# A fourth split weight tile in the place of the activations, and one more block with another order of products

## The chip, the cores and the metric

One Trainium2 chip, one of its cores. The metric is the device time of one execution of the whole kernel in microseconds (us). Engines: PE = TensorE, DVE = VectorE, ACT = ScalarE, POOL = GpSimd, SP = SyncE; PEld is the loading of weights into TensorE.

## The reference

The kernel computes one decoder layer, all in float32: 256 tokens and 16 meta tokens in front of them, 2048 channels. An attention half and a pooling half are mixed and normalised; then comes a gated feed-forward part with 5632 channels, whose time this text is about:

```
h = layer_norm(ALPHA * h + mix, ln1_g, ln1_b)
z = h @ w_up                                  # 2048 -> 2 x 5632
z = causal depthwise conv of width 3 over the tokens, + conv_b
a, g = split(z, 2)
f = (gelu(a) * g) @ w_down                    # 5632 -> 2048
h = layer_norm(ALPHA * h + f, ln2_g, ln2_b)   # meta tokens are dropped
```

## The kernel before

**Weights.** All weights come as tiles of 128 partitions and 2048 float32 columns, 1 MB each, in one list, `stream`. A float32 matmul is done as three products of a faster format: each operand is written as an upper part (rounded) and a lower part (the rest), and the products upper·upper, upper·lower and lower·upper are added. So each tile is loaded by SP's queue (L190) into a raw buffer `wraw`, ACT copies its upper part into a split buffer `whl` (L184), and DVE subtracts that from the raw tile for the lower part (L185). A tile is split in two or three parts (`cuts`): 512 and 1536 columns for a tile of `w_up`, 1024 and 1024 for an A tile of `w_down`, 1024, 512 and 512 for a B tile. There are three raw and three split buffers (pool `wp`). `weights` hands out the next tile and emits the work for tiles up to two ahead.

**Feed-forward part.** `ffn_plan` lists the work. A tile of `w_up` ("up") makes one block of 128 output channels: 16 steps of three products with 258 columns each, 48 in all (L295). `b` counts these blocks, from -8; `lead(b)` says in which order the three products of a step come in the first step: "l" is the lower part of the weights by the upper part of the activations, "x" the upper part by the lower, "h" upper by upper. Two up blocks (a and g) pass through `conv` (ACT L824, DVE L825 and L826) and `gate` (ACT L841, DVE `za` L842). A tile of `w_down` is used in a scheme of seven block products instead of eight: an A tile takes part in four of them, a B tile in three, each with three matmuls of 512 columns (`seven`, L893 to L895), so 12 and 9. Four A tiles, then four B tiles, and so on in turn; up tiles and down tiles alternate one by one. The seven products need sums of blocks of the weights (DVE L196 for an A tile, L200, L201, L202 for a B tile, made in the raw buffer) and of the activations: `forms` makes the latter on POOL after every second pair of blocks (L866 to L869, in the program's text s[0], s[2], s[1], s[3]), and `two_parts` splits them (ACT L847, DVE L848; tiles `gp` and `right`).

**PSUM.** The up blocks use the four buffers of pool `pm`, the down products the four of `pa` (tile `at`). At the end of four A tiles ACT copies two sums (`u` L907, `v` L909) and DVE adds two to the output (`y<-y,at`, L903); at the end of four B tiles DVE does `y<-y,v`, `u` (L917), `y<-y,at` and `v` (L918). POOL's queue then adds `u` and `v` to the output with accumulating transfers (L912, L913; L920 to L922). These two places are called hand-overs here, from A to B and from B to A tiles.

**Order.** The instructions of each engine run in order. That order is set when the kernel is built, by a scheduler that takes the program's dependences, the free buffers and its own idea of durations; `issue_after` in the text adds edges that it must keep.

**The place.** The tile of tag "y" first holds x, then the normalised activations. After the normalisation, 32 transfers (`residual`, L817, on ACT's queue, called from the loop over the plan) move these to the output's buffer `y2`; the list of those still to come is `moves`. After that nothing uses the place until tile number `spare`, near the end of the stream, whose split tile `whl_y` lies there.

Of the kernel before, what the change touches and what calls it, by code (L numbers as in the profile page):

```python
# [12 lines left out]
F32R = mybir.dt.float32r  # L13
# [4 lines left out]
P = 128  # L18
# [84 lines left out]

def lead(b):

    if 8 < b < 16:
        return (), ("lxh",)
    return (), ()

# [14 lines left out]
def places(n):  # L124

    upper, apart, turned = WAYS[(n >= 8) + (n >= 26) + (n >= 26 + KT)]
    return upper, upper + apart, turned
# [8 lines left out]
def tile_layer(ctx, tc, xt, w_first, w_proj, w_uk, w_uv, w_pool, w_o, w_up, w_down, cols, rows, rel_bias, onehot, out):  # L136
    nc = tc.nc
    sb = ctx.enter_context(tc.tile_pool(name="sb", bufs=1))
# [23 lines left out]
    kinds, leads, downs_at = {}, {**{i: LEAD_X for i in (10, 14)}, **{26 + m: LEAD_H for m in (0, 1, 5)}}, {}  # L162
# [12 lines left out]
    spare, last = len(stream) - PARTS[-1], len(stream) - 1  # L175
    VALUES = stream.index(w_uv)
    ready, raws, split, held = {}, {}, {}, []
    state = {"next": 0, "use": 0}

    def split_part(raw, hl, c, after=()):  # L180
        with ExitStack() as edges:
# [6 lines left out]
    def fetch(raw, hl, src, kind, front, at_up=False):  # L188

        nc.sync.dma_start(raw, src)  # L190
        b11, b12, b21, b22 = (raw[:, c:c + 512] for c in range(0, 2048, 512))
        cuts = (0, 1024, 2048)
        if kind == "A":

            with tc.issue_after(front):
                nc.vector.tensor_tensor(b12, b12, b11, op=ALU.subtract)  # L196
        if kind == "B":

            with tc.issue_after(front):
                nc.vector.tensor_tensor(b12, b22, b12, op=ALU.subtract)  # L200
            nc.vector.tensor_tensor(b11, b12, b11, op=ALU.add)  # L201
            nc.vector.tensor_tensor(b21, b21, b11, op=ALU.subtract)  # L202
            cuts = (0, 1024, 1536)
        if hl.lead is not None or kind is None and at_up:
            cuts = (0, hl.first or 512, 2048)
        for a, b in zip(cuts, cuts[1:]):
            parts = split_part(raw, hl, slice(a, b))
        return parts

    def split_tile(where=(0, 2048)):  # L210

        return Split(wp.tile([P, 4288], F32R, tag="whl", name="whl"), *where)

    def weight_tiles(where):
        raw = wp.tile([P, 2048], F32, tag="wraw", name="wraw")
        return raw, split_tile(where)

    def emit(i):
        if i in ready:
            return  # L220
        if i == last:

            raw = wp.tile([P, 2048], F32, tag="wraw", name="wraw")
            nc.sync.dma_start(raw, stream[i])
            raws[i] = raw
            ready[i] = []
            for c in range(0, 2048, 256):
                hl = ring.tile([P, 2, 258], F32R, tag="act", name="whl_r", padded_shape=[P, 2, WIDE])
                nc.scalar.activation(hl[:, 0, :256], raw[:, c:c + 256], AF.Copy)
                nc.vector.tensor_tensor(hl[:, 1, :256], raw[:, c:c + 256], hl[:, 0, :256].bitcast(F32), op=ALU.subtract)  # L230
                ready[i].append(hl)
            return
        if i == spare:
            raw = wp.tile([P, 2048], F32, tag="wraw", name="wraw")
            hl = Split(sb.tile([P, 4160], F32R, tag="y", name="whl_y"), 0, 2056)
        else:
            raw, hl = weight_tiles((0, 2112) if i > spare else downs_at.get(i, places(i)) + leads.get(i, ()))
        ready[i] = hl
        if i == VALUES:

            nc.sync.dma_start(raw, stream[i])
            held.extend((raw, hl))
            return
        split[i] = fetch(raw, hl, stream[i], kinds.get(i), i and i - 1 in split and split[i - 1][1], i in orders)
        if i >= spare:
            raws[i] = raw
# [6 lines left out]
    def weights(ahead=2):  # L253
        i = state["use"]
        state["use"] += 1
        prefetch(i + 1 + ahead)
        return ready.pop(i)
# [44 lines left out]
    for k0, k1 in [(k, k + 1) for k in range(9)] + [(9, 12), (12, 15), (15, 16)]:  # L302
        if k0 == KT - 1:

            raw = ap_.tile([P, 1024], F32, name="wraw_l", tag="v1")[:, :T + MF].rearrange("p (a b) -> p a b", a=1)
        elif k0 % 3 == 0:
            raw = wp.tile([P, 2048], F32, tag="wraw", name="wraw")
            raw = raw[:, :3 * (T + MF)].rearrange("p (a b) -> p a b", b=T + MF)
        if k0 % 6 == 0:
            hl = split_tile()  # L310
# [155 lines left out]
    for j in range(8):  # L466
        hl = weights()
# [39 lines left out]
    y = sb.tile([P, KT, T], F32, tag="y", name="x", padded_shape=[P, KT, T])  # L507
# [50 lines left out]
    for h in range(H):  # L558
        hl = weights()
# [127 lines left out]
    for h in range(H):  # L687
# [3 lines left out]
        hl = weights()  # L691
# [121 lines left out]
    def residual(a, b, i):  # L813

        src, dst, t = slice(32 * a, 32 * a + 32), slice(32 * b, 32 * b + 32), NM + i * P + 32 * b
        to = y2[dst, i, :].rearrange("p (m d) -> p m d", d=P)[:, :, src]
        nc.scalar.dma_start(to, y[src, :, t:t + 32])  # L817

    turns = list(range(KT))
    moves = [(a, b, i) for i in range(2) for a in range(4) for b in range(4)]  # L820
# [106 lines left out]
    for item in plan:  # L927
        if item[0] in "AB":
            seven(*item)
            continue  # L930
        if item[0] == "down":
            _, part, c, g = item
            hl = weights()
            if c == 1:
                emit((last, spare)[g])
                if g == 0:
                    row_sums(last, ready[last])
            if g == 0:
                downs = [big(), big()]
            n = PARTS[part]  # L940
            for k in range(4 * g, 4 * g + 4):
                w = slice(512 * (k - 4 * g), 512 * (k - 4 * g) + 512)
                for i in range(2):
                    a, r = pairs[part][k // 2][f"a{i + 1}{k % 2 + 1}"]
                    nc.tensor.matmul(downs[i], a[:, 0, r], hl[:, 0, w], start=k == 0, stop=False)
                    nc.tensor.matmul(downs[i], a[:, 0, r], hl[:, 1, w], start=False, stop=False)
                    nc.tensor.matmul(downs[i], a[:, 1, r], hl[:, 0, w], start=False, stop=k == n - 1)
            if g == n // 4 - 1:
                for i in range(2):
                    yc = y2[:, i, 512 * c:512 * c + 512]  # L950
                    nc.vector.tensor_tensor(yc, yc, downs[i], op=ALU.add)
            continue
        _, f, half_ = item
        part = next(p for p in range(len(PARTS)) if f < sum(PARTS[:p + 1]))
        if half_ == 0:
            if f % 2 == 0:
                pair = fp.tile([P, 2, S], F32, name="za", tag="z0", bufs=3)
            both = []
        hl = weights()
        ps = big()  # L960

        b = 2 * (f - FOLDED) + half_
        upper, lower = split[state["use"] + 1]
        with tc.issue_after(lower):
            for m in turns[:(0, 5, 5, 6)[b] if 0 <= b < 4 else 0]:
                nc.vector.transpose(y[:, m, NM:], y[:, m, NM:])
                turns.remove(m)
        with tc.issue_after(upper):
            for _ in range(0 if b < 4 else 4 if b < 8 else 3):
                if moves:  # L970
                    residual(*moves.pop(0))
        if todo and f > FOLDED + half_:
            p, r = todo.pop(0)
            with behind(state["use"]):
                pairs[p].append(forms(r, len(pairs[p]), p == FAST))
        if f < FOLDED:
            k = 0
            if f + half_ == 0:
                product(ps[:, :NE], hl, folded, 0, NE, K_UP, k1=5)
                deviation()  # L980
                k = 5
            product(ps[:, :NE], hl, folded, 0, NE, K_UP, k0=k)
            with behind(state["use"]):
                while len(h_parts) < min(KT, 2 * (2 * f + half_ + 1) + 3):
                    normalise(len(h_parts))
            both.append(ps)
            if half_ == 0:
                continue
            both = [conv(i * FT + f, i, unfold(both[i]), pair[:, f % 2]) for i in range(2)]
        else:  # L990
            product(ps[:, :NQ], hl, h_parts, 0, NQ, K_UP, ks=late_last if f == FOLDED else None,
                    firsts=orders[state["use"] - 1])
            both.append(conv(half_ * FT + f, half_, ps, pair[:, f % 2]))
            if half_ == 0:
                continue
        gate(*both)
        if part > FAST:
            a = fp.tile([P, 2, WIDE], F32R, name="gp", tag="gp", bufs=16)
            gated.append(two_parts(a[:, :, :S], both[0]))
        elif f % 2:  # L1000
            todo.append((part, pair))
# [192 lines left out]
```

## Time and profile before

| | us |
|---|---|
| Runs, median of 3 | 1021.62 (1021.62 to 1033.16) |
| Profiled execution, its own time | 1020.11 |
| Its span, first to last instruction | 1018.3 |
| PE busy | 1011.5 |
| DVE busy | 889.9 |
| ACT busy | 621.2 |

The mean granted clock of TensorE in this execution is 0.997 of full speed. The profile shows one execution: busy times by engine, groups of instructions by line, waits with the engine that ended them, and a timeline. All times further down count from the start of the span. The feed-forward part's alternating stretch lies between about 320 and 965 us. In the timeline, successive instructions of one group stand in one row with their number (x2), and the time is from the first's start to the last's end.

### The profile page before, as it was taken

What the parts mean: (1) busy time and instruction counts of PE and PEld (TensorE: products, weight loads), DVE (VectorE), ACT (ScalarE), POOL (GpSimd) and SP (SyncE); (2) the same over time, 40 slices, a digit from 0 to 9 for tenths busy, and PEclk for the clock granted to TensorE, in tenths of its full rate; (3) what the DMA queues carried; (4) which work ended last, traced back from release to release, by engine and by line L of the source; (5) the groups of instructions that cost most, each with busy time, mean ns of one, the idle gap of its engine ahead of it and who ended that gap; (6) DMA issues with size and microseconds to landing.
All of it is one profiled execution on the core that took longest, in us unless ns stands there. A gap on an engine that the chain in (4) does not pass through costs nothing.

```text
span 1018.3 us, 19199 instructions
## 1 busy us (share of the span) xinstructions
PE 1011.5 (99%) x7644; PEld 963.5 (95%) x7644; DVE 889.9 (87%) x1401; ACT 621.2 (61%) x1000; POOL 187.5 (18%) x245
## 2 busy tenths in 40 slices
PE   9999999999999999999999999999999999999997
PEld 8999999999999999999999999999999999999986
DVE  6878678758879999999998999989999899999976
ACT  7666446655548756655666656656555656565675
POOL 1200014125430021111121111210212102120031
PEclk9999999999999999999999999999999999999998
DMA  8755643354663568979888798878988888888874
GB/s 325 259 190 209 236 156 105 138 196 166 207 207 125 207 208 263 267 291 309 273 288 272 281 302 275 279 262 299 284 269 289 281 296 287 276 291 282 298 229 155
DMA packets 59754, 250.28 MB, mean 246 GB/s; under 512 B 21734, under 2 KB 22416, under 8 KB 32656
## 3 DMA queue, kind: packets, MB, share of 16 engines
q1 hardware_dynamic: 34592, 230.42, 62.8%
q0 software_dynamic: 7888, 16.14, 8.3%
q10 hardware_dynamic: 17184, 2.49, 1.5%
q8 instruction: 60, 0.98, 0.4%
q14 instruction: 30, 0.25, 0.1%
HBM read 232.50 MB, written 2.11 MB: 230 GB/s over the span
## 4 chain that ended last, share of the span: by engine, by line
PE 59%; DVE 20%; DMA 8%; ACT 7%; issue 4%; POOL 1%; SPq 0%; ACTq 0%; POOLq 0%; DVEq 0%
PE mm L295 46%; DVE whl L185 11%; ACT whl L184 6%; DMA wraw<-in_w_up 5%; DMA wraw<-in_w_down 3%; PE at L894 2%; PE at L893 2%; PE at L895 2%; PE mm L366 1%; DVE y L903 1%; DVE wraw L201 1%; DVE wraw L200 1%; DVE wraw L196 1%; DVE gp L848 1%; DMA wraw<-in_w_first 1%
## 5 line engine op out<-in xcount | busy, mean ns | idle before, releaser
L185 DVE TENSOR_TENSOR whl<-wraw,whl 128x1024 fp32r<-128x1024 f32 (+2 forms) x416 | 487.3, 1199 | 51.7 <-ACT whl L184 50.2
L184 ACT ACTIVATE whl<-wraw 128x1024 fp32r<-128x1024 f32 (+2 forms) x416 | 401.9, 1014 | 172.1 <-DVE wraw L201 45.6
L295 PEld LDWEIGHTS mm<-hp,whl 128*128 128x128 f32 x3840 | 456.9, 188 | 6.3
L295 PE MATMUL mm<-hp,whl 128*128 128x258 f32 x3840 | 458.9, 279 | 0.0
L295 PE MATMUL mm<-xp,whl 128*128 128x256 f32 (+5 forms) x1152 | 147.0, 284 | 0.0
L295 PEld LDWEIGHTS mm<-xp,whl 128*128 128x128 f32 x1152 | 140.1, 188 | 1.5 <-issue 0.5
L866 POOL TENSOR_TENSOR forms<-za 128x128 f32<-128x128 f32 x20 | 20.3, 1017 | 294.9 <-DVE za L842 230.2
L894 PE MATMUL at<-whl,gp 128*128 128x512 f32 x180 | 70.6, 393 | 0.0
L895 PE MATMUL at<-whl,gp 128*128 128x512 f32 x180 | 70.4, 392 | 0.0
L893 PE MATMUL at<-whl,gp 128*128 128x512 f32 x180 | 68.7, 392 | 0.0
L869 POOL TENSOR_TENSOR forms<-za 128x128 f32<-128x128 f32 x20 | 19.0, 949 | 201.3 <-DVE za L842 187.5
L824 ACT ACTIVATE z<-mm,cv 128x256 f32<-128x256 f32 x40 | 22.5, 562 | 51.6 <-PE mm L295 51.5
L295 PE MATMUL mm<-mixp,whl 128*128 128x258 f32 x384 | 48.0, 280 | 0.0
L295 PE MATMUL mm<-mixa,whl 128*128 128x258 f32 x384 | 47.2, 279 | 0.0
L295 PEld LDWEIGHTS mm<-mixp,whl 128*128 128x128 f32 x384 | 46.1, 188 | 0.1
L295 PE MATMUL mm<-fold,whl 128*128 128x260 f32 x384 | 45.8, 280 | 0.0
L824 ACT ACTIVATE za<-mm,cv 128x256 f32<-128x256 f32 x40 | 22.4, 561 | 38.1 <-PE mm L295 36.7
L295 PEld LDWEIGHTS mm<-mixa,whl 128*128 128x128 f32 x384 | 45.7, 188 | 0.0
L295 PEld LDWEIGHTS mm<-fold,whl 128*128 128x128 f32 x384 | 45.5, 187 | 0.1
L895 PEld LDWEIGHTS at<-whl,gp 128*128 128x128 f32 x180 | 33.9, 188 | 7.2
L894 PEld LDWEIGHTS at<-whl,gp 128*128 128x128 f32 x180 | 33.8, 188 | 6.1
L893 PEld LDWEIGHTS at<-whl,gp 128*128 128x128 f32 x180 | 33.4, 187 | 6.2
(329 smaller groups left out, 1277.9 us busy)
## 6 DMA issues: line engine op xcount, KB each, us to landing
wraw<-in_w_up SPq DMA_DIRECT2D x88, 1024.0 KB, 5.1
wraw<-in_w_down SPq DMA_DIRECT2D x80, 1024.0 KB, 6.2
wraw<-in_w_proj SPq DMA_DIRECT2D x24, 1024.0 KB, 4.9
wraw<-in_w_o SPq DMA_DIRECT2D x16, 1024.0 KB, 4.8
y<-v POOLq DMA_DIRECT2D x27, 256.0 KB, 8.3
y<-u POOLq DMA_DIRECT2D x18, 256.0 KB, 4.9
wraw<-in_w_first SPq DMA_DIRECT2D x8, 304.0 KB, 5.7
x<-in_xt SPq DMA_DIRECT2D x1, 2176.0 KB, 8.0
```

Source lines behind the costliest of these rows:

```text
L184: upper = nc.scalar.activation(hl[:, 0, c], raw[:, c], AF.Copy)
L185: lower = nc.vector.tensor_tensor(hl[:, 1, c], raw[:, c], hl[:, 0, c].bitcast(F32), op=ALU.subtract)
L196: nc.vector.tensor_tensor(b12, b12, b11, op=ALU.subtract)
L200: nc.vector.tensor_tensor(b12, b22, b12, op=ALU.subtract)
L201: nc.vector.tensor_tensor(b11, b12, b11, op=ALU.add)
L295: nc.tensor.matmul(ps, a, b, start=n == 0 and i == 0, stop=i == 2 and n == KT - 1)
L824: nc.scalar.activation(z, src[:, 2:NQ], AF.Identity, bias=col(C_B, j), scale=col(C_W, 3 * j + 2))
L866: nc.gpsimd.tensor_tensor(s[:, 0], a21, a22, op=ALU.add)
L869: nc.gpsimd.tensor_tensor(s[:, 3], a11, a21, op=ALU.subtract)
L893: nc.tensor.matmul(ps, a[:, 0, i], hl[:, 0, w], start=j == 0, stop=False)
L894: nc.tensor.matmul(ps, a[:, 0, i], hl[:, 1, w], start=False, stop=False)
L895: nc.tensor.matmul(ps, a[:, 1, i], hl[:, 0, w], start=False, stop=j == n - 1)
```

## The change

Two edits. Block 16 gets the order of its first step that the blocks 9 to 15 have. And once the list of moves is empty, a tile `whl_y` of the size of a split buffer is allocated in the place "y"; from then on the split tile of every fourth raw tile is that one instead of one of the three `whl`, up to four tiles before `spare`. In the program that is built, 33 weight tiles have it, each second of the down tiles among them. In the changed file the lines of `fetch` and `split_part` stand one lower (L185 is L186), those of the feed-forward part four lower (L842 is L846, L866 is L870).

```
--- before.py
+++ after.py
@@ -103,7 +103,7 @@
 
 def lead(b):
 
-    if 8 < b < 16:
+    if 8 < b < 17:
         return (), ("lxh",)
     return (), ()
 
@@ -175,7 +175,8 @@
     spare, last = len(stream) - PARTS[-1], len(stream) - 1
     VALUES = stream.index(w_uv)
     ready, raws, split, held = {}, {}, {}, []
-    state = {"next": 0, "use": 0}
+    state = {"next": 0, "use": 0, "raw": 0}
+    more = []
 
     def split_part(raw, hl, c, after=()):
         with ExitStack() as edges:
@@ -211,8 +212,11 @@
 
         return Split(wp.tile([P, 4288], F32R, tag="whl", name="whl"), *where)
 
-    def weight_tiles(where):
+    def weight_tiles(where, i):
         raw = wp.tile([P, 2048], F32, tag="wraw", name="wraw")
+        state["raw"] += 1
+        if more and i < spare - 4 and state["raw"] % 4 == 0:
+            return raw, Split(more[0], *where)
         return raw, split_tile(where)
 
     def emit(i):
@@ -234,7 +238,7 @@
             raw = wp.tile([P, 2048], F32, tag="wraw", name="wraw")
             hl = Split(sb.tile([P, 4160], F32R, tag="y", name="whl_y"), 0, 2056)
         else:
-            raw, hl = weight_tiles((0, 2112) if i > spare else downs_at.get(i, places(i)) + leads.get(i, ()))
+            raw, hl = weight_tiles((0, 2112) if i > spare else downs_at.get(i, places(i)) + leads.get(i, ()), i)
         ready[i] = hl
         if i == VALUES:
 
@@ -969,6 +973,8 @@
             for _ in range(0 if b < 4 else 4 if b < 8 else 3):
                 if moves:
                     residual(*moves.pop(0))
+        if not (moves or more):
+            more.append(sb.tile([P, 4288], F32R, tag="y", name="whl_y"))
         if todo and f > FOLDED + half_:
             p, r = todo.pop(0)
             with behind(state["use"]):
```

The order of instructions on SP and on PE stays, but for the names and block 16. On DVE, ACT and POOL it changes in most of the stretch. First DVE at a hand-over from A to B tiles in the later part of the stretch, before:

```order
L842 TENSOR_TENSOR za<-za,z 128x256
L185 TENSOR_TENSOR whl<-wraw,whl 128x512
L903 SCALAR_TENSOR_TENSOR y_3782<-y_3782,at 128x512 x2
L185 TENSOR_TENSOR whl<-wraw,whl 128x512
L185 TENSOR_TENSOR whl<-wraw,whl 128x1536
L848 TENSOR_TENSOR gp<-za,gp 128x256
L848 TENSOR_TENSOR gp<-forms,gp 128x256
L848 TENSOR_TENSOR right<-forms,right 128x256
L848 TENSOR_TENSOR gp<-za,gp 128x128
```

and after, at the same kind of place:

```order
L829 SCALAR_TENSOR_TENSOR z<-mm,cv,z 128x256
L907 SCALAR_TENSOR_TENSOR y_3782<-y_3782,at 128x512
L830 SCALAR_TENSOR_TENSOR z<-mm,cv,z 128x256
L907 SCALAR_TENSOR_TENSOR y_3782<-y_3782,at 128x512
L846 TENSOR_TENSOR za<-za,z 128x256
L186 TENSOR_TENSOR whl<-wraw,whl 128x512
L186 TENSOR_TENSOR whl<-wraw,whl 128x1536
L852 TENSOR_TENSOR gp<-za,gp 128x256
L852 TENSOR_TENSOR gp<-forms,gp 128x256
L852 TENSOR_TENSOR right<-forms,right 128x256
L852 TENSOR_TENSOR gp<-za,gp 128x128
```

The two adds that read PSUM (`y<-y,at`) stood behind `za`, and a 512 part of an up tile before and behind them; they now stand ahead of `za`, and both parts of the up tile follow it, with `gp` behind them.

DVE at a hand-over from B to A tiles, before:

```order
L842 TENSOR_TENSOR za<-za,z 128x256
L185 TENSOR_TENSOR whl<-wraw,whl 128x1024
L903 SCALAR_TENSOR_TENSOR y_3782<-y_3782,v 128x512
L917 TENSOR_TENSOR u<-u,at 128x512
L903 SCALAR_TENSOR_TENSOR y_3782<-y_3782,at 128x512
L918 TENSOR_TENSOR v<-u,at 128x512
L185 TENSOR_TENSOR whl<-wraw,whl 128x512
L185 TENSOR_TENSOR whl<-wraw,whl 128x1536
L848 TENSOR_TENSOR gp<-za,gp 128x256
L848 TENSOR_TENSOR gp<-forms,gp 128x256
L848 TENSOR_TENSOR right<-forms,right 128x256
```

and after:

```order
L921 TENSOR_TENSOR u<-u,at 128x512
L846 TENSOR_TENSOR za<-za,z 128x256
L922 TENSOR_TENSOR v<-u,at 128x512
L907 SCALAR_TENSOR_TENSOR y_3782<-y_3782,at 128x512
L186 TENSOR_TENSOR whl<-wraw,whl 128x1536
L852 TENSOR_TENSOR gp<-za,gp 128x256
L852 TENSOR_TENSOR gp<-forms,gp 128x256
L852 TENSOR_TENSOR right<-forms,right 128x256
L852 TENSOR_TENSOR gp<-za,gp 128x128
```

`u` moved ahead of `za`; the 1024 part of a down tile and the 512 part of an up tile, which stood behind `za`, are done before it (so is `y<-y,v`, above these rows), and `v` comes ahead of the add. In the changed order `gp` follows two adds and one 1536 part.

POOL over one hand-over of each kind, first from A to B, then from B to A (rows named DMA issue the accumulating transfers), before:

```order
L869 TENSOR_TENSOR forms<-za 128x128
L866 TENSOR_TENSOR forms<-za 128x128
L867 TENSOR_TENSOR forms<-forms,za 128x128
L868 TENSOR_TENSOR forms<-za,forms 128x128
L912 DMA y_3782<-u 128x512
L913 DMA y_3782<-v 128x512
L869 TENSOR_TENSOR forms<-za 128x128
L866 TENSOR_TENSOR forms<-za 128x128
L867 TENSOR_TENSOR forms<-forms,za 128x128
L868 TENSOR_TENSOR forms<-za,forms 128x128
L920 DMA y_3782<-u 128x512
L921 DMA y_3782<-v 128x512
```

and after:

```order
L916 DMA y_3782<-u 128x512
L917 DMA y_3782<-v 128x512
L870 TENSOR_TENSOR forms<-za 128x128
L871 TENSOR_TENSOR forms<-forms,za 128x128
L872 TENSOR_TENSOR forms<-za,forms 128x128
L873 TENSOR_TENSOR forms<-za 128x128
L924 DMA y_3782<-u 128x512
L870 TENSOR_TENSOR forms<-za 128x128
L926 DMA y_3782<-v 128x512
L925 DMA y_3782<-v 128x512
L871 TENSOR_TENSOR forms<-forms,za 128x128
L872 TENSOR_TENSOR forms<-za,forms 128x128
```

L869 (now L873) was the first of its group, far ahead of the others in time since it needs only the first of the two `za`, and is the last; the two transfers at the end of A tiles stand ahead of `forms`, and at the end of B tiles two of the three transfers stand between its first and its second operation.

## Rows read from the trace of the kernel before

**Rows 1.** The page's part 1: busy us (share of the span) x instructions.
```profile
PE 1011.5 (99%) x7644; PEld 963.5 (95%) x7644; DVE 889.9 (87%) x1401; ACT 621.2 (61%) x1000; POOL 187.5 (18%) x245
```

**Rows 2.** Windows: busy us (x instructions) of each engine, PE clock, DMA share, GB/s.
```profile
core 0: us, PE busy (x) PEld busy (x) DVE busy (x) ACT busy (x) POOL busy (x), PEclk, DMA share, GB/s
...
450.00:960.00 510.00, 510.00 (x3734) 481.73 (x3734) 479.74 (x658) 310.44 (x434) 81.97 (x99) 1.00 0.85 285
```

**Rows 3.** Waits of SyncE's queue, whole span: total us, times, longest.
```profile
SPq L190 <- DVE whl L185: 661.6, 165, 13.8
```

**Rows 4.** Waits of DVE, 450 to 960 us.
```profile
DVE whl L185 <- ACT whl L184: 19.4, 44, 2.4
```

**Rows 5.** Waits of ACT, 450 to 960 us.
```profile
ACT gp L847 <- POOL forms L868: 8.6, 11, 1.3
```

**Rows 6.** Timeline, A to B hand-over: start, us, engine, line, operation, count.
```profile
486.56 0.42 DVE L842 TENSOR_TENSOR za<-za,z 128x256 f32<-128x256 f32 x1
...
486.89 0.68 DVE L185 TENSOR_TENSOR whl<-wraw,whl 128x512 fp32r<-128x512 f32 x1
487.06 0.85 POOL L866 TENSOR_TENSOR forms<-za 128x128 f32<-128x128 f32 x1 [14.80 <-DVE za L842]
...
487.50 1.28 DVE L903 SCALAR_TENSOR_TENSOR y<-y,at 128x512 f32<-128x512 f32 x2
...
487.98 0.47 POOL L867 TENSOR_TENSOR forms<-forms,za 128x128 f32<-128x128 f32 x1
488.53 0.46 POOL L868 TENSOR_TENSOR forms<-za,forms 128x128 f32<-128x128 f32 x1
...
489.32 0.41 ACT L847 ACTIVATE gp<-forms 128x256 fp32r<-128x256 f32 x1
...
491.46 0.41 DVE L848 TENSOR_TENSOR gp<-forms,gp 128x256 fp32r<-128x256 f32 x1
```

**Rows 7.** Timeline, B to A hand-over at 840 to 845 us.
```profile
839.64 1.22 DVE L185 TENSOR_TENSOR whl<-wraw,whl 128x1024 fp32r<-128x1024 f32 x1
839.80 1.38 POOL L866 TENSOR_TENSOR forms<-za 128x128 f32<-128x128 f32 x1 [12.15 <-DVE za L842]
...
842.13 0.39 PE L893 MATMUL at<-whl,gp 128*128 128x512 f32 x1
...
842.36 0.39 PE L894 MATMUL at<-whl,gp 128*128 128x512 f32 x1
...
842.84 0.67 DVE L918 TENSOR_TENSOR v<-u,at 128x512 f32<-128x512 f32 x1
...
843.44 2.35 DVE L185 TENSOR_TENSOR whl<-wraw,whl 128x512 fp32r<-128x512 f32 x2
...
843.82 0.85 POOL L921 DMA_DIRECT2D y<-v  x1 [0.33 <-DVE v L918]
...
844.10 1.05 ACT L184 ACTIVATE whl<-wraw 128x1024 fp32r<-128x1024 f32 x1
844.19 0.40 PE L893 MATMUL at<-whl,gp 128*128 128x512 f32 x1
...
844.36 1.20 POOL L922 DMA_DIRECT2D y<-v  x1
...
844.89 1.35 PE L295 MATMUL mm<-hp,whl 128*128 128x258 f32 x10
```

**Rows 8.** Groups of DVE by line and shape, 450 to 960 us: busy, mean ns, idle before.
```profile
L185 DVE TENSOR_TENSOR whl<-wraw,whl 128x1024 fp32r<-128x1024 f32 x96 | 115.7, 1219 | 4.6 <-ACT whl L184 4.1
L185 DVE TENSOR_TENSOR whl<-wraw,whl 128x1536 fp32r<-128x1536 f32 x64 | 113.5, 1774 | 9.1 <-ACT whl L184 8.8
...
L202 DVE TENSOR_TENSOR wraw<-wraw 128x512 f32<-128x512 f32 x32 | 22.0, 688 | 0.9
```

**Rows 9.** Windows of PE alone, up blocks 15 and 16.
```profile
383.31:388.91 5.60, 5.60 (x50) 1.00 0.71 181
388.91:394.57 5.66, 5.66 (x50) 1.00 1.09 288
```

More of the change, by code (lines that the diff above doesn't have):

```diff
@@ L104, in lead @@
 def lead(b):
-    if 8 < b < 16:
+    if 8 < b < 17:
         return (), ("lxh",)
@@ L177, in tile_layer @@
     ready, raws, split, held = {}, {}, {}, []
-    state = {"next": 0, "use": 0}
+    state = {"next": 0, "use": 0, "raw": 0}
+    more = []
     def split_part(raw, hl, c, after=()):
@@ L212, in split_tile, with weight_tiles @@
         return Split(wp.tile([P, 4288], F32R, tag="whl", name="whl"), *where)
-    def weight_tiles(where):
+    def weight_tiles(where, i):
         raw = wp.tile([P, 2048], F32, tag="wraw", name="wraw")
+        state["raw"] += 1
+        if more and i < spare - 4 and state["raw"] % 4 == 0:
+            return raw, Split(more[0], *where)
         return raw, split_tile(where)
@@ L236, in emit @@
         else:
-            raw, hl = weight_tiles((0, 2112) if i > spare else downs_at.get(i, places(i)) + leads.get(i, ()))
+            raw, hl = weight_tiles((0, 2112) if i > spare else downs_at.get(i, places(i)) + leads.get(i, ()), i)
         ready[i] = hl
@@ L971, in tile_layer @@
                     residual(*moves.pop(0))
+        if not (moves or more):
+            more.append(sb.tile([P, 4288], F32R, tag="y", name="whl_y"))
         if todo and f > FOLDED + half_:
```

## Prediction

> **What bounds the kernel now.** I read the page's busy times first: the reader is to see TensorE (PE) at 99% of the span [rows 1]. A share is an average, so next the windows: between 450 and 960 us, the stretch in which up and down tiles alternate and the fourth weight tile works, PE is busy 510.00 of 510 us at full granted clock, and VectorE (DVE) 479.74 [rows 2]. Does late weight data hold PE back there in a way that busy time hides? No: two successive products of 512 columns start at 842.13 and 842.36, 0.23 us apart, 2.2 columns per ns [rows 7]; an up tile has 48 products of 258 columns and takes 5.60 us, again 2.2 per ns [rows 9]. PE streams columns at one rate without gaps. Earlier weights can't make it faster.
>
> Then the waits. SyncE waits 661.6 us for `whl<-wraw` of DVE [rows 3]: the next raw tile is loaded when DVE has finished with one of the three raw buffers. The change adds a split buffer and no raw one, so loads stay paced by DVE. DVE itself is idle 30.3 of the 510 us, and 19.4 of that it waits for ACT's half of a split [rows 4]; the other 10.9 are small waits for loads and `conv`, and hand-offs. So it is nearly a second bound. The timeline shows how near: the row at 843.44 joins the two parts of an up tile's weights, 512 and 1536 columns, and the second leaves DVE at 843.44 + 2.35 = 845.79; PE began that tile at 844.89 [rows 7] and its first twelve products use the first part. It needs the second at 844.89 + 12 × 0.117 = 846.29, half a us later.
>
> **The change part by part.** *Block 16.* Blocks with the first three products as "lxh" take 5.60 us, block 16 without it 5.66 [rows 9]: minus 0.06.
>
> *The fourth split tile.* It takes away a wait of ACT for PE to release a `whl`. In the stretch nothing late hangs on that: SyncE waits for raw tiles [rows 3], and PE for nothing [rows 2]. Gain 0. The 33 tiles at the other address could be read at another rate. The nearest row for such a difference is block 16's 1%; on 33 tiles of 2 to 6 us that is about ±1.5 us. The three addresses of today have one rate, so I take 0. The place's first use must wait for the 32 moves out of it, issued blocks ahead: 0.
>
> *The order.* With a buffer more the scheduler puts the instructions of DVE, ACT and GpSimd (POOL) in another order through the whole stretch, and this can cost. After every four up tiles, in turn at the hand-over from A to B tiles and from B to A, `za` (L842) is followed by `forms` on POOL, their upper parts on ACT (L847) and the lower parts on DVE (L848).
>
> How does POOL fare beside DVE? L866 takes 0.85 us under a DVE split that reads two SBUF operands, ending 0.34 after the split (487.91 against 487.57), and 1.38 under a longer split, ending 0.32 after it. Beside adds that read PSUM, L867 and L868 take 0.47 and 0.46 [rows 6, 7]. A `forms` operation waits out the split. The Trainium skill, "SBUF — State Buffer", section "Who interferes with whom", says that a DVE instruction with two SBUF inputs and a GpSimd instruction that reads SBUF exclude each other for the whole instruction; the trace agrees, 0.85 and 1.38 against 0.46 us. By that rule the sum is the one below; were the access shared, each chain would be about 1 us shorter and the sum some 10 us less.
>
> In the old order, from A to B, two PSUM-reading adds stand behind `za` and POOL's chain runs beside them; `gp<-forms` comes on DVE 491.46 − 486.98 = 4.5 us after `za` ended [rows 6]. In the new order the adds stand ahead of `za`, so behind it come a 512 split, a 1536 split and then `gp`. Counted from `za`'s end: the splits end at 0.70 + 1.77 = 2.5 [rows 6, 8], `gp<-za` at 2.9. POOL: L866 until 0.9 as in the row; L867 starts under the 1536 split and ends 0.33 behind it, 2.8; L868 and L869 follow at the step of 0.55 (488.53 − 487.98), 3.9. L869 stood ahead of the other three, at the `za` before, and is last now, and on ACT `right<-forms` stands ahead of `gp<-forms`: 0.41 each, 4.8 [rows 6]. DVE stands idle from 2.9 to 4.8: 1.9 us. The transfers `y<-u`, `y<-v`, which POOL's queue now has ahead of the chain, can only make it later: 2.0. Behind the waiting DVE instruction stand `right`, the next B tile's combinations and its splits, so every later weight is late by as much.
>
> From B to A two adds (0.67 each [rows 7]) and the 1536 split stand behind `za`: 3.1, and `gp<-za` 3.5. POOL has two transfers between L866 and L867, 0.85 and 1.20 [rows 7], released by `v`. L867 falls under the 1536 split: it ends at 3.4, L869 at 4.5, ACT at 5.3: 1.8 us. If POOL goes on before a transfer is over, 1.4. I take 1.6. Six hand-overs of each kind in the stretch have this order (the first four stay near the old one): 6 × 2.0 + 6 × 1.6 = 21.6 us. Bounds: 0, if `forms` slips in ahead of the splits, and 12 × 2.8, the whole chain after its first 2.0 us.
>
> *B tiles.* The 1024 split now follows L202 directly. ACT's part needs L201 and then 1.05 us [rows 7]; L202 covers 0.69 of it [rows 8], so DVE waits 0.4 us; 32 tiles, 13 us, less the 4.1 that it waits for this form today [rows 8]: 9. In the old order `conv` operations stand between in about half of them. Between 0 and 9 I take 4.5.
>
> *Sum.* DVE's busy time with its 19.4 us for ACT, which come from the order within a tile and stay, is 499.1. Plus 21.6 and 4.5: 525.2 against PE's 510, thus 15.2 over. The other 10.9 us of idle I take to vanish once DVE is behind; if they stay, it is 26. On the profiled execution's 1020.11: 1020.11 + 15.2 − 0.06 = 1035. The median of the runs, 1021.62, is 1.5 us more; a median could stand as much above my number, which the range holds.
>
> **The rivals.** *The cover holds.* The 30.3 us of DVE's idle time absorb the 26.1 of new stalls, since a DVE that is late waits for no one: 479.74 + 26.1 = 505.8, and PE stays at 510: 1020 to 1022. For it: PE waits for nothing today. Against: the 19.4 are for ACT, which itself needs DVE's combinations of the same tile, and half a us of cover at 846.29.
>
> *Slower by more than 2%.* Nothing bends: today's idle stays, all twelve hand-overs cost 2.0 and the B tiles 9: 510 + 24 + 9, so 33 over. From B to A the release of PSUM is late as well: today `v` is read out at 843.51 and PE takes that bank at 844.19, 0.68 later [rows 7]; the new order has `za` and an add ahead of it. With three quarters of this it is 1045, with all 1053. It decides once the new DVE idle that bends nowhere passes 20 us.
>
> *Faster.* If the fourth tile's address reads faster by as much as the order of the first triple saves on a tile, 0.06 us [rows 9], the 33 tiles give 2 us: 1018. The Trainium skill, "Perfetto Trace Analysis", section "Identifying the Most-Contended Engine", calls matmul busy time a bad measure and wants the weight loads' busy share: 481.73 of 510 [rows 2], which would leave 28 us and give 992. The trace speaks against it: loads idle where 512-column products set the pace, and these run at 2.2 columns per ns like the others.
>
> **How the numbers follow.** The likeliest, DVE as the bound by its stalls behind `forms`: 0.60, 1027 to 1042. The cover holds: 0.20. Slower by over 2% (20.4 us, so above 1042; 2% is also about what a measurement here tells from no change): 0.15 by its own case and 0.03 from the upper end of the likeliest. Faster: 0.05, 0.02 of it over 2%. The range goes from 1019, where the cover holds, to 1047, in the middle of the slow case.
>
> **What would show it.** Right: DVE waits 15 us or more for ACT on `gp` or `right`, ACT's wait for POOL's `forms` grows from 8.6 us [rows 5], PE waits for DVE's `whl` behind 500 us, and the medians of L866 to L868 (then L870 to L872) are above 1 us. PE's window up to 450 is as before, and block 16 takes 5.60. Wrong: PE stays at 510.00 of 510 with DVE's idle only moved (cover), or PE waits at the A and B products for PSUM instead of weights.

## The result, and the profile after

The changed kernel takes 1035.37 us (median, 1032.36 to 1038.33); before took 1021.44 (1019.69 to 1033.16) in the same set of runs. The ratio is 1.0121, 95% interval 1.0098 to 1.0144: 14 us more by the medians, 12 by the ratio. The profiled execution took 1036.95 us, its span is 1035.2, 16.9 more than before's 1018.3. (Lines in the changed file: L186 is the lower part of a split, L185 the upper; L846 `za`; L852 and L851 the lower and upper parts of `gp` and `right`; L870 to L873 `forms`; L897 to L899 the A and B products.)

Where do the 16.9 us lie? Windows of the changed kernel (us; then busy time and instructions of PE, PEld, DVE, ACT and POOL; PE's clock, DMA share, GB/s):

```profile
32.00:387.00 355.00, 354.87 (x2950) 349.53 (x2949) 287.93 (x548) 212.05 (x402) 79.36 (x98) 1.00 0.53 186
...
450.00:975.00 525.00, 520.11 (x3736) 483.78 (x3735) 482.48 (x657) 308.98 (x432) 99.55 (x99) 1.00 0.83 276
```

and one window of before that answers to the first:

```profile
30.00:385.00 355.00, 354.88 (x2950) 349.55 (x2949) 287.97 (x548) 212.18 (x402) 79.42 (x98) 1.00 0.54 186
```

From 32 to 387 the changed kernel does what before does from 30 to 385, with the same 2950 products. So 2 us come from the first 30 us, where no instruction differs, so they are not the change's. (Another execution of the changed kernel, profiled in run 8, has a span of 1031.4.) From 450 on, 525 us hold 3736 products, where before 510 us held 3734 [rows 2]: the other 15 us. DVE's busy time is 482.48 against 479.74, its idle time 42.5 against 30.3.

The blocks 15 and 16, windows of PE alone (compare [rows 9]):

```profile
385.32:390.92 5.60, 5.60 (x51) 1.00 0.73 185
390.92:396.52 5.60, 5.60 (x50) 1.00 1.08 292
```

Block 16 has lost its 0.06 us. Now the waits between 450 and 975 us, the three largest of DVE (total us, times, longest):

```profile
DVE gp L852 <- ACT gp L851: 16.9, 14, 2.6
DVE whl L186 <- ACT whl L185: 13.6, 21, 2.7
DVE whl_y L186 <- ACT whl_y L185: 8.6, 16, 0.5
```

then the two of ACT for POOL's `forms`:

```profile
ACT right L851 <- POOL forms L871: 41.2, 14, 3.8
...
ACT gp L851 <- POOL forms L872: 2.4, 8, 1.1
```

In [rows 4] DVE had 19.4 us for `whl`, and none for `gp`. A wait for `gp` has come, 16.9 us; behind it ACT's wait for POOL, 8.6 us in [rows 5], is 41.2 + 2.4. The waits for split tiles are 13.6 + 8.6 = 22.2. PE, which waited for nothing:

```profile
PE at L898 <- DVE whl L186: 2.1, 2, 1.4
PE at L897 <- DVE u L921: 1.3, 4, 0.4
PE at L897 <- ACT whl L185: 0.7, 1, 0.7
PE mm L299 <- DVE whl L186: 0.2, 1, 0.2
```

This list holds 4.3 us of the 15, since a product that starts late counts as busy. So I added up, over all products from 385 to 975 us, the time from one's start to the next one's, less the even pace of before (0.1162 us for a product of an up tile, 0.230 for one of a down tile). Before this is about 0 in all, now 14.8: 8.9 in down tiles, 5.9 in up tiles, nearly all of it behind 530 us. 4.8 of it lie in the six A tiles that come first at a hand-over from B to A; most of the rest follows a hand-over from A to B or lies in up tiles. The largest single piece, 1.8 us, is in the A tile at 533 us, behind DVE's longest wait for `gp`, 2.6.

The timeline of the changed kernel at one hand-over from A to B (start, us, engine, line, operation), to be read beside [rows 6]:

```profile
560.25 0.42 DVE L846 TENSOR_TENSOR za<-za,z 128x256 f32<-128x256 f32 x1
...
560.59 2.91 DVE L186 TENSOR_TENSOR whl<-wraw,whl 128x512 fp32r<-128x512 f32 x2
...
560.88 1.03 POOL L917 DMA_DIRECT2D y<-v  x1
...
561.44 2.36 POOL L870 TENSOR_TENSOR forms<-za 128x128 f32<-128x128 f32 x1
...
563.88 0.54 POOL L871 TENSOR_TENSOR forms<-forms,za 128x128 f32<-128x128 f32 x1
564.45 0.42 ACT L851 ACTIVATE right<-forms 128x256 fp32r<-128x256 f32 x1 [3.32 <-POOL forms L871]
564.49 0.46 POOL L872 TENSOR_TENSOR forms<-za,forms 128x128 f32<-128x128 f32 x1
...
565.44 0.43 DVE L852 TENSOR_TENSOR gp<-forms,gp 128x256 fp32r<-128x256 f32 x1 [1.35 <-ACT gp L851]
...
568.93 0.50 PE L897 MATMUL at<-whl,right 128*128 128x512 f32 x1 [0.70 <-ACT whl L185]
...
570.19 0.51 PE L898 MATMUL at<-whl,right 128*128 128x512 f32 x1 [0.76 <-DVE whl L186]
```

`za` ends at 560.67. The 512 and the 1536 split run from 560.59 to 563.50, and L870, started under them, ends 0.30 us behind, at 563.80, after 2.36 us. Then come L871, L872 and ACT's `gp<-forms`. DVE starts its `gp<-forms` at 565.44, 4.8 us after `za`'s end, having stood 1.35 us. The B tile's first part comes late behind it: PE's first product of that tile waits 0.70 for it, the next 0.76.

At a hand-over from B to A, beside [rows 7]:

```profile
593.51 0.39 PE L897 MATMUL at<-whl_y,gp 128*128 128x512 f32 x1
...
594.01 0.67 DVE L921 TENSOR_TENSOR u<-u,at 128x512 f32<-128x512 f32 x1
...
594.60 0.41 DVE L846 TENSOR_TENSOR za<-za,z 128x256 f32<-128x256 f32 x1
...
594.73 0.50 PE L897 MATMUL at<-whl_y,gp 128*128 128x512 f32 x1 [0.36 <-DVE u L921]
...
595.59 0.74 POOL L870 TENSOR_TENSOR forms<-za 128x128 f32<-128x128 f32 x1
...
595.99 1.17 POOL L926 DMA_DIRECT2D y<-v  x1
...
596.13 1.82 DVE L186 TENSOR_TENSOR whl<-wraw,whl 128x1536 fp32r<-128x1536 f32 x1
...
596.58 1.47 POOL L925 DMA_DIRECT2D y<-v  x1
...
597.14 1.40 POOL L871 TENSOR_TENSOR forms<-forms,za 128x128 f32<-128x128 f32 x1
...
597.88 0.95 DVE L852 TENSOR_TENSOR gp<-za,gp 128x256 fp32r<-128x256 f32 x1
...
599.63 0.42 DVE L852 TENSOR_TENSOR gp<-forms,gp 128x256 fp32r<-128x256 f32 x1 [0.80 <-ACT gp L851]
```

POOL's two transfers (595.99, 596.58) lie between L870 and L871. L871 falls under the 1536 split, and takes 1.40 us. DVE's `gp<-za` behind the split is itself held up, 0.95 us instead of 0.41. At the same time `u` is read out of PSUM at 594.01 only, half a us behind the start of the A tile, and the fourth product waits for that bank, 594.73 instead of 594.21.

Two groups of POOL's `forms` and four of DVE, 450 to 975 us (count, busy, mean ns, idle before):

```profile
L870 POOL TENSOR_TENSOR forms<-za 128x128 f32<-128x128 f32 x15 | 23.4, 1560 | 14.4 <-DVE za L846 14.4
L871 POOL TENSOR_TENSOR forms<-forms,za 128x128 f32<-128x128 f32 x15 | 15.7, 1047 | 0.6
```

```profile
L186 DVE TENSOR_TENSOR whl<-wraw,whl 128x1536 fp32r<-128x1536 f32 x64 | 116.0, 1812 | 1.4 <-ACT whl L185 1.4
L186 DVE TENSOR_TENSOR whl_y<-wraw,whl_y 128x1024 fp32r<-128x1024 f32 x48 | 58.6, 1221 | 9.2 <-ACT whl_y L185 8.6
L186 DVE TENSOR_TENSOR whl<-wraw,whl 128x1024 fp32r<-128x1024 f32 x48 | 58.3, 1220 | 7.7 <-ACT whl L185 7.6
...
L852 DVE TENSOR_TENSOR gp<-za,gp 128x256 fp32r<-128x256 f32 x18 | 11.6, 647 | 0.0
```

and the last of them before, 450 to 960 us:

```profile
L848 DVE TENSOR_TENSOR gp<-za,gp 128x256 fp32r<-128x256 f32 x18 | 7.4, 413 | 0.0
```

L870 and L871 take 1560 and 1047 ns on average; L866 and L867 took 1129 and 640 between 450 and 960 us. The split forms have kept their means to within 40 ns of [rows 8]; `gp<-za` has gone from 413 to 647 ns. The 1024 splits now wait 8.6 + 7.6 for ACT, 4.1 before, and the 1536 splits 1.4, where it was 8.8.

### The profile page after: what moved, and what is told of

The parts are those of the page before. It is cut to its first block, busy times and chain, and to the rows that moved or that the text cites. A ratio compares the mean times of both kernels' runs of the same rounds, so it can differ in the third digit from the quotient of the medians.

```text
span 1035.2 us, 19311 instructions
## 1 busy us (share of the span) xinstructions
PE 1022.0 (99%) x7644; PEld 966.5 (93%) x7644; DVE 892.0 (86%) x1401; ACT 620.2 (60%) x1000; POOL 205.7 (20%) x245
## 5 line engine op out<-in xcount | busy, mean ns | idle before, releaser
L299 PE MATMUL mm<-hp,whl 128*128 128x258 f32 x3840 | 463.6, 280 | 0.2 <-DVE whl L186 0.2
L186 DVE TENSOR_TENSOR whl<-wraw,whl 128x1024 fp32r<-128x1024 f32 (+1 forms) x350 | 421.4, 1224 | 45.9 <-ACT whl L185 45.3
L185 ACT ACTIVATE whl<-wraw 128x1024 fp32r<-128x1024 f32 (+1 forms) x350 | 345.0, 1029 | 140.3 <-DVE wraw L202 33.2
L185 ACT ACTIVATE whl_y<-wraw 128x1024 fp32r<-128x1024 f32 x68 | 63.2, 948 | 74.2 <-DVE wraw L202 49.3
L186 DVE TENSOR_TENSOR whl_y<-wraw,whl_y 128x1024 fp32r<-128x1024 f32 x68 | 73.2, 1087 | 12.2 <-ACT whl_y L185 11.6
L873 POOL TENSOR_TENSOR forms<-za 128x128 f32<-128x128 f32 x20 | 34.6, 1728 | 220.1 <-DVE za L846 220.1
L870 POOL TENSOR_TENSOR forms<-za 128x128 f32<-128x128 f32 x20 | 26.8, 1340 | 102.4 <-DVE u L841 47.7
L898 PE MATMUL at<-whl,gp 128*128 128x512 f32 x99 | 39.0, 395 | 1.4 <-DVE whl L186 1.4
L899 PE MATMUL at<-whl,gp 128*128 128x512 f32 x99 | 38.6, 392 | 0.0
L897 PE MATMUL at<-whl,gp 128*128 128x512 f32 x99 | 37.1, 392 | 0.0
L897 PE MATMUL at<-whl_y,gp 128*128 128x512 f32 x81 | 32.9, 406 | 1.7 <-DVE u L921 1.3
L851 ACT ACTIVATE right<-forms 128x256 fp32r<-128x256 f32 x20 | 8.3, 413 | 41.2 <-POOL forms L871 41.2
L898 PE MATMUL at<-whl_y,gp 128*128 128x512 f32 x81 | 31.8, 393 | 0.0
```

Source lines behind the costliest of these rows:

```text
L185: upper = nc.scalar.activation(hl[:, 0, c], raw[:, c], AF.Copy)
L186: lower = nc.vector.tensor_tensor(hl[:, 1, c], raw[:, c], hl[:, 0, c].bitcast(F32), op=ALU.subtract)
L299: nc.tensor.matmul(ps, a, b, start=n == 0 and i == 0, stop=i == 2 and n == KT - 1)
L851: nc.scalar.activation(a[:, 0], src, AF.Copy)
L870: nc.gpsimd.tensor_tensor(s[:, 0], a21, a22, op=ALU.add)
L873: nc.gpsimd.tensor_tensor(s[:, 3], a11, a21, op=ALU.subtract)
```

## The experiments

Theory 1: the loss is the order that the scheduler sets with a fourth tile. At the hand-overs the `forms` chain over POOL and ACT runs into DVE's splits, DVE stands before `gp`, and it has no slack for that. Theory 2: the tile in that place costs by itself, in being written, read or waited for. A third would lay it to block 16.

**1. Block 16 alone.** The fourth tile is never taken:

```
-        if more and i < spare - 4 and state["raw"] % 4 == 0:
+        if False and more and i < spare - 4 and state["raw"] % 4 == 0:
```

> Only the order of block 16's first step; no fourth split tile. All theories: 0.06 us less than before, which can't be told from it: 1021.4 us, ratio 0.998 to 1.002. PE has no waits between 450 and 960 us; block 16 takes 5.60 us where it took 5.66.

1020.63 us, ratio 0.9982 (0.9965 to 0.9998). PE has no wait in the stretch. The change's first edit costs nothing. The 0.18% is more than the 0.06 us that the trace shows, and lies at the edge of what the runs resolve.

**2. The fourth tile alone.**

```
-    if 8 < b < 17:
+    if 8 < b < 16:
```

> Only the fourth split tile; block 16 as before. All theories that put the loss on the tile or on the order it brings: as the full change, 1034 to 1037 us. If the order of block 16's products had a part in the loss: clearly less than that.

1032.41 us, ratio 1.0088 (1.0062 to 1.0114): most of the loss, though 3 us less than the full change by the medians. Runs 8 to 10 come back to that.

**3. The place used, the old order.** The scheduler's order depends on which tiles go there. With every eighth raw tile and remainder 0 all hand-overs keep the order of before, from `za` to `gp`, on DVE, and POOL's order is the same as before throughout:

```
-        if more and i < spare - 4 and state["raw"] % 4 == 0:
+        if more and i < spare - 4 and state["raw"] % 8 == 0:
```

> The fourth tile takes every eighth raw tile instead of every fourth. POOL's order is that of before, and at all hand-overs DVE's order from za to gp is that of before. Theory 1 (the loss is the order at the hand-overs, not the tile): 1020 to 1023 us, DVE waits for ACT on gp under 3 us between 450 and 975, PE without gaps. Rival theory 2 (each tile in the place costs, in being written, read or waited for): half of the loss stays, about 1028 us.

1020.95 us, ratio 0.9992 (0.9975 to 1.0009). The window from 450 to 960 and the products of the second line of a down tile, from either place:

```profile
450.00:960.00 510.00, 510.00 (x3734) 481.73 (x3733) 476.53 (x656) 309.30 (x433) 80.93 (x99) 1.00 0.86 285
```

```profile
L898 PE MATMUL at<-whl,gp 128*128 128x512 f32 x121 | 47.5, 393 | 0.0
...
L898 PE MATMUL at<-whl_y,gp 128*128 128x512 f32 x40 | 15.7, 393 | 0.0
```

PE is busy 510.00 of 510 again, and products from the place take 393 ns as those from the others do. Theory 2 falls for these tiles.

**4. The fourth tile as in the change, the adds behind `za`.** An edge holds the adds of finished sums (L907) behind the last `za` on DVE:

```
+        g = nc.vector.tensor_tensor(za, za, zg, op=ALU.mult)
+        held["gate"] = getattr(g, "ins", g)
...
-            with tc.issue_after(split[min(state["use"] + 1, last - 1)][1]):
+            with tc.issue_after(split[min(state["use"] + 1, last - 1)][1]), tc.issue_after(held["gate"]):
```

From A to B DVE now has `za`, two adds, a 1536 split, `gp`; from B to A three adds, the split, `gp`. POOL makes `forms` ahead of its transfers from A to B, and ahead of those of `v` from B to A.

> The full change with the fourth tile as it is, but the adds of the finished PSUM sums to the output are held behind za on DVE; with that POOL makes forms ahead of its transfers from A to B. Theory 1: the chain over POOL and ACT runs beside the adds again, DVE's wait for ACT on gp falls from 16.9 to under 5 us, the stalls of PE behind a hand-over from A to B go; left are what the B tiles' order costs and the release of PSUM from B to A: 1022 to 1027 us. Theory 2: 1035 us as the full change.

1025.19 us, ratio 1.0027 (1.0008 to 1.0046). DVE's waits, 450 to 975 us:

```profile
DVE whl L186 <- ACT whl L185: 19.6, 23, 2.2
...
DVE gp L853 <- ACT gp L852: 3.7, 15, 0.8
```

The wait for `gp` falls from 16.9 to 3.7 us and ten of the 14 us are gone (by the medians), with the same tiles in the place. By the sum over starts 5.2 us of delay at PE stay in the profile, 3.1 of them in A tiles behind B to A.

**5. The same from A to B alone.** The edge is drawn only where `kind == "A"`.

> As the run with the adds behind za, but only at the hand-overs from A to B; from B to A the order is that of the full change. Theory 1: the stalls of PE for weights behind A-to-B hand-overs go, those for the release of PSUM from B to A (six times 0.6 to 1.0 us, 4.8 in all) and half of DVE's wait on gp (about 9 us) stay: 1026 to 1030 us. Theory 2 (the tile itself costs): 1035 us.

1025.71 us, ratio 1.0021 (0.9999 to 1.0042); in the profile DVE still waits 9.8 us for `gp`. PE's delay is 2.2 us, all in A tiles behind B to A, where I expected 4.8: with DVE earlier from the hand-over before, `u` and `v` are read out sooner as well. So the late release of PSUM was for about half a consequence of a late DVE (4.8 us in one profile, 2.2 in the other). And 9.8 us of waits for `gp` remain without any delay in up or B tiles: about that much seems to fit into DVE's slack.

**6. About as many tiles as in run 3, a new order.** `% 8 == 3` instead of `% 8 == 0`. 16 tiles have the place, 17 in run 3. They are all up tiles, where those of run 3 and of the change are down tiles: the two runs differ in the kind of tile as well as in the order.

> The fourth tile takes every eighth raw tile, as in the third run, but those with another remainder: now the scheduler sets at all 14 later hand-overs one add, the 512 and the 1536 split between za and gp, and a transfer between POOL's first and second forms operation. As many tiles lie in the place as in the third run. Theory 1: DVE waits 12 to 20 us for ACT on gp, and the time is 1028 to 1035 us. Theory 2: as the third run, 1021 us.

1039.59 us, ratio 1.0159 (1.0105 to 1.0212), 4.6 us above the range that I gave. The wait of DVE for `gp`, and the products of up tiles from either place, 450 to 975 us:

```profile
DVE gp L852 <- ACT gp L851: 26.7, 15, 2.7
```

```profile
L299 PE MATMUL mm<-hp,whl 128*128 128x258 f32 x2276 | 274.5, 279 | 0.8 <-DVE whl L186 0.7
L299 PE MATMUL mm<-hp,whl_y 128*128 128x258 f32 x768 | 91.8, 279 | 0.0
```

With half the change's tiles in the place the loss is as large or larger. It is 18 us more than run 3, 17 when each is taken against before in its own set. Products of up tiles from the place take 279 ns as the others do, and DVE's 1536 splits into it 1753 ns against 1789, so up tiles are neither read nor written more slowly there. What is left for the difference is the order.

**7. Three tiles, nothing of the change, only `forms` late.** In the kernel before, POOL's first `forms` operation is held behind the last transfer of the finished tiles:

```
-        nc.gpsimd.tensor_tensor(s[:, 0], a21, a22, op=ALU.add)
+        with ExitStack() as edges:
+            if "moved" in held:
+                edges.enter_context(tc.issue_after(held["moved"]))
+            nc.gpsimd.tensor_tensor(s[:, 0], a21, a22, op=ALU.add)
...
+        held["moved"] = getattr(moved, "ins", moved)
```

> The kernel before, three split tiles, nothing of the change; only POOL's first forms operation is held behind the transfers of the finished tiles, so that the chain over POOL and ACT comes about 1.5 us later on DVE at each of 16 hand-overs. Theory 1: DVE waits 10 to 24 us for gp, the slack of DVE is used up and PE stalls: 1027 to 1037 us. Theory 2, and any that needs the fourth tile: 1021 us.

1028.71 us, ratio 1.0058 (1.0038 to 1.0078). DVE's waits, the timeline of one hand-over, and a window of PE alone behind it:

```profile
DVE gp L848 <- ACT gp L847: 16.1, 15, 1.5
DVE whl L185 <- ACT whl L184: 11.8, 36, 1.2
```

```profile
686.88 1.21 POOL L869 TENSOR_TENSOR forms<-za 128x128 f32<-128x128 f32 x1
...
689.27 0.42 ACT L847 ACTIVATE gp<-forms 128x256 fp32r<-128x256 f32 x1
...
689.73 0.43 DVE L848 TENSOR_TENSOR gp<-forms,gp 128x256 fp32r<-128x256 f32 x1 [1.34 <-ACT gp L847]
...
693.47 0.50 PE L896 MATMUL at<-whl,right 128*128 128x512 f32 x1 [0.95 <-ACT whl L184]
...
694.73 0.70 PE L897 MATMUL at<-whl,right 128*128 128x512 f32 x1 [0.76 <-DVE whl L185]
```

```profile
694.86:698.27 3.41, 3.41 (x9) 0.50 0.56 171
```

A late chain alone makes DVE wait 16.1 us for `gp` and costs 5.5 us without a fourth tile. By the sum over starts PE is 6.6 us late in this profile, and 3.8 of that lie at the hand-over shown: PE's next B tile starts late, 0.95 us by its own row, its second product 0.76. Behind these two waits TensorE's granted clock is at half of full speed (1.2 instead of 2.4 GHz) for 3.41 us, and products start 0.43 us apart instead of 0.23: about 1.6 of the 6.6 us are this clock. In the changed kernel, behind the like waits at 568.93 and 570.19, it stayed at full speed.

As much waiting for `gp` as in the change costs less than half as much here. The waits for `whl` fell to 11.8 us at the same time. The first A tiles behind B to A, 4.8 us late in the change, are on time here, where the order of `u` and `v` is that of before; the second A tiles lose 1.7 us. That this is the whole difference isn't shown.

**8 to 10. Scatter or block 16?** The full change, then the fourth tile alone and the full change once more on one chip.

> The full change once more, beside the others on the same chip: 1032 to 1036 us. If the 3 us by which the run with the fourth tile alone lay under it belong to block 16, it is again 3 us over 1032.4; if they are scatter, it may come out at either.

1036.51 us, ratio 1.0142 (1.0119 to 1.0164).

> The fourth tile alone, timed again beside the full change on one chip. The order of instructions is that of the full change on every engine, and block 16's order changes 0.06 us. If the difference seen so far (1032.4 against 1035 to 1037 us) is scatter of late loads, the two agree within their intervals; if block 16 matters, this one is again 3 to 4 us lower.

1035.04 us, ratio 1.0139 (1.0122 to 1.0156).

> The full change, timed beside the fourth tile alone on one chip: 1033 to 1037 us; the same as that one if the difference so far is scatter, 3 to 4 us above it if block 16 matters.

1036.64 us, ratio 1.0157 (1.0139 to 1.0175). The intervals overlap and the tile alone has come up to 1035: the 3 us of run 2 were scatter for the larger part. A difference of 1 to 2 us isn't excluded. The two sets of the tile alone, 1.0088 and 1.0139, lie further apart than their intervals, so half a per cent between two sets can be scatter. Run 7's 0.6% is hardly more: that a late chain alone costs time rests on its profile as well as on its time.

No version beats both kernels by more than the runs resolve; run 1 and run 3 equal before.

## Why the prediction was right, point by point

**What bounds the kernel.** Right. PE had nothing to gain, and DVE became the bound: PE waits for DVE's parts, and the time is got back when DVE's wait for `gp` goes (run 4). Of the stretch's 525 us DVE is busy 482.5, waits 16.9 for `gp` and 22.2 for split tiles, and is otherwise idle 3.4. (Busy and idle time add up to 525 in any case; the terms are what can be compared.) The prediction had 479.7, 21.6, 23.9 and 0. That its sum is 525.2 is partly luck: 4.7 and 1.7 us too much against 2.7 (in which lie the 4.2 of `gp<-za` below) and 3.4 too little.

**Block 16 and the tile.** Right: 5.66 became 5.60, and run 3 shows the place as neutral. The possible ±1.5 us for its reading rate did not appear: 393 ns from either place.

**The chain at the hand-overs.** The mechanism was right, and the 21.6 us nearly: DVE's wait for `gp` is 16.9 us, and `gp<-za` with its mean of 647 instead of 413 ns, slow while POOL works, adds 18 × 0.234 = 4.2: 21.1. But the total is made up otherwise. The six hand-overs from A to B wait 1.34 to 1.89 us each, 8.6 in all, and the six from B to A 0.80, 4.8 in all, where 2.0 and 1.6 were forecast. The other 3.4 of the 16.9 us come from the two hand-overs ahead of them, near 492 and 526 us, which I had taken to stay near the old order. So the nearness of the total is luck. Of the steps two were wrong, and their errors cancelled. From A to B, L869 (now L873) is not the last of its group: it runs at the `za` before, as it did, and I had read the transfers between as a border between groups (the section on the change calls it the last, too); and `right<-forms` ahead of `gp<-forms` on ACT costs nothing, because ACT does it while POOL is still at L872 (564.45 and 564.49). These are 0.55 and 0.41 us too much. In their place stands what I had put at 0.1: the transfers ahead of L870 held it until 561.44, so that L870 and not L871 waited out the splits. The end, 4.8 us after `za`, is as predicted. From B to A the end came 599.63 − 595.01 = 4.6 after `za`, predicted 5.3, by the same two steps. Medians of L870 to L872 above 1 us, which I had named as a sign, were a poor one: at either hand-over shown only one of the three is blocked (L870 for 2.36, L871 for 1.40 us), so between 450 and 975 us the medians are 1.38, 0.80 and 0.47, and L866's was 1.38 before. The means show it.

**B tiles.** The 4.5 us were mis-sized as a term of the sum. The waits of the 1024 splits grew by 12.1 us, more than the 9 that I had as the most (DVE's idle time ahead of those of B tiles went from 1.7 to 15.5), but those of the 1536 splits fell by 7.4 and of the 512 ones by 1.9: waits for `whl` together grew from 19.4 to 22.2, 2.8 us. Run 5, where the B tiles have the new order, has no delay in them.

**What vanishes.** Of the 10.9 us of other idle time 3.4 are left (42.5 − 16.9 − 22.2): taken to vanish, it mostly did.

**The rivals.** The cover did not hold, though run 5 shows that a part of it does. The release of PSUM, which I had left to the slow case, is there: 4.8 of PE's 14.8 us. By run 5 about half of it follows from DVE's lateness, a place where the 15 us show and no addition to them; whether the other half is an addition isn't shown. In run 6 the first A tiles are on time, and the loss is as large without it. Faster did not come.

**Not settled.** That POOL waits out a DVE split of two SBUF operands is read from durations (an end 0.30 to 0.34 us after the split's at 487.91, 841.18 and 563.80, but 0.59 at 598.54; 0.46 to 0.74 us for an operation beside other work); no run took the shared access away. The Trainium skill, "SBUF — State Buffer", section "Who interferes with whom", says that either one blocks the other: that DVE is held up as well shows in `gp<-za`, 0.95 us from 597.88 while L871 runs until 598.54.

## What to carry to other kernels

Where an engine beside the bound is 94% busy, a buffer that no one waits for can still cost, because it lets a scheduler reorder that engine's queue. Here an edge that put two or three adds back behind `za` returned ten of 14 us (run 4). Compare the order at the places where a short chain crosses engines, and ask of each operation in it what will run beside it. Before a number is given to a chain, follow which group each of its operations belongs to, and when its inputs are ready.

## What was not expected

Runs 3 and 6 put about as many tiles in the same place and differ by 18 us: the remainder of a count by eight decided between 1021 and 1040 us. It chose down tiles in one and up tiles in the other, and neither kind is read more slowly from there; what the remainder changed besides is the order.

The wait for `gp` and the loss are not in proportion. It is 16.9 to 17.4 us in the three profiles of the change, which are 1031.4 to 1035.2 us long; 16.1 us cost 5.5 in run 7, and 9.8 us in run 5 left up and B tiles on time.
